# Down-projection weights of a two-layer decoder trunk: their two halves built by GpSimd-issued DMAs instead of by a load and VectorE

## The chip, the cores and the metric

The kernel runs on one core of a Trainium2 chip. TensorE (PE in the profile, with PEld for its weight loads), VectorE (DVE), ScalarE (ACT), GpSimd (POOL) and SyncE (SP, which here only issues DMAs) run side by side, each through its own instruction queue in order, and wait for each other by semaphores. The metric is the device time of one execution in microseconds, lower is better; the time before is the median of three runs.

## What is computed

Two layers over 512 tokens of width 1024, all in float32. Each layer is: half-step SwiGLU FFN, a mixer (layer 0 a Conformer convolution, layer 1 sparse attention), a second half-step SwiGLU FFN, and a gated per-layer embedding; at the end one RMSNorm. Cut to what matters here:

```
def swiglu(x, wg, wu, wd):                 # wg, wu: 1024 x 2816, wd: 2816 x 1024
    return (silu(x @ wg) * (x @ wu)) @ wd

for i in range(2):
    x = x + 0.5 * swiglu(rms_norm(x, ffn1_norm[i]), ffn1_w_gate[i], ffn1_w_up[i], ffn1_w_down[i])
    x = x + (conformer_conv if i == 0 else nsa_mixer)(rms_norm(x, mix_norm[i]), ...)
    x = x + 0.5 * swiglu(rms_norm(x, ffn2_norm[i]), ffn2_w_gate[i], ffn2_w_up[i], ffn2_w_down[i])
    x = x + sigmoid(rms_norm(x, ple_norm[i]) @ ple_w_gate[i]) * (p[i] @ ple_w_in[i])
return rms_norm(x, final_norm)
```

The four FFNs (two a layer) hold four down matrices `w_down`; they are what the change is about.

## The kernel before

**Products.** The matmuls take fp32r, a rounded form of float32. To keep the precision, every operand is split into a high part h (the value rounded to fp32r) and a low part l (the value minus h, rounded), and each product is three matmuls: h·h, h·l and l·h, in this order, in `mm3` (lines 349, 350, 351). The weight block of 128 x 128 is the stationary operand, so lines 349 and 350 load `wh` and line 351 loads `wl`.

**Weights.** The host packs all 128 x 128 weight blocks in the order of use into units of eight (128 x 1024 float32, 512 KB); `plan` lists the units and gives each a kind. Kind "s" is the plain one: `_load` fetches the unit with a DMA from SP's queue into one of two `raw` buffers (line 243), and `_split` lets ScalarE copy it rounded into `wh` (line 291) and VectorE, or GpSimd for some names, subtract `wh` from `raw` into `wl` (line 292). Kinds "a" and "b" are pairs of units of the gate and up matrices; these products go by a seven-product scheme (`pairs`), for which `first_sums` and `combine` form sums of blocks and split them (lines 305 to 324). Kind "r" is loaded raw.

**Buffers and order.** There are five `wh` and five `wl` buffers (HLB = 5), used in rotation by the splits. `block` is asked for each weight block; it calls `ahead`, which writes down the splits up to five entries beyond the one in use (fewer while `held` blocks are still needed) and, through `loads`, the loads of the units that come next. A split can run when the unit that had its buffers five splits earlier is used up. The instructions are written down in this order; when the program is built, a planner with a model of the chip's timing arranges each engine's queue by when it thinks that things are ready, the earlier written first.

**An FFN.** The 22 blocks f of the inner width are cut into parts of 8, 8 and 6. In each part the gate and up products of all its f are computed (in pairs f, f+1, with ScalarE copying sums out of PSUM at line 496 and VectorE adding at line 495 between the products), SiLU and the product with up give `hid` (its split is at lines 551 to 554), and then the down products: for each m of the eight output blocks, sum over the part's f of `w_down[f, m]` times `hid[f]`, 128 x 512 outputs (24 matmuls for a unit of eight blocks). The first two m are interleaved: all but the last two f of m = 0, the same of m = 1, then the last two f of both. VectorE adds each finished m to the residual (lines 605, 606). A part's down blocks are 8 units (6 in the third part), so an FFN has 22 down units and the kernel 88, in twelve parts.

Beside this, GpSimd issues few DMAs of its own (line 1289: eight stores of 256 KB from SBUF to DRAM; some small loads), and it computes the low parts for `ple_w_gate`, `conv_w_pw2` and the attention weights, the reciprocal roots of the norms, and parts of the convolution and the attention.

Of the kernel before, what the change touches and what calls it, by code (L numbers as in the profile page):

```python
# [11 lines left out]
F32 = mybir.dt.float32  # L12
F32R = mybir.dt.float32r
I32 = mybir.dt.int32
AF = mybir.ActivationFunctionType
OP = mybir.AluOpType
# [40 lines left out]
def plan():  # L57
    units, kinds = [[]], ["s"]
    place = {}

    def put(key, rows, cols, kind="s"):
        w = sum(b - a for a, b in cols)
        used = sum(x[2] for x in units[-1])
        if used + w > HU or kinds[-1] != kind:
            units.append([])
            kinds.append(kind)
            used = 0
        place[key] = (len(units) - 1, used, w)
        units[-1].append((key, used, w, rows, cols))

    def ffn(n, i):
        for fs in PARTS:
            order = [(nm, f) for f in fs if f < PLAIN for nm in ("gate", "up")]
            for f in fs:
                if f >= PLAIN and f % 2 == 0:
                    order += [("gate", f), ("gate", f + 1), ("up", f), ("up", f + 1)]
            for nm, f in order:
                for k in range(KD):
                    put((f"ffn{n}_w_{nm}", i, k, f), k, ((f * 128, f * 128 + 128),), "ab"[f % 2] if f >= PLAIN else "s")
            for m in range(KD):  # L80
                for f in fs:
                    put((f"ffn{n}_w_down", i, f, m), f, ((m * 128, m * 128 + 128),))

    def full(name, i, kk, ms):
        for m in ms:
            for k in range(kk):
                put((name, i, k, m), k, ((m * 128, m * 128 + 128),))

    def conv(i):
        for c in range(KD):  # L90
            for o in (c, c + KD):
                for k in range(KD):
                    put(("conv_w_pw1", i, k, o), k, ((o * 128, o * 128 + 128),))
        for z in range(L):
            full("ple_w_in", z, PLE // 128, range(KD))
        for ms in (range(0, 4), range(4, 8)):
            for k in range(KD):
                for m in ms:
                    put(("conv_w_pw2", i, k, m), k, ((m * 128, m * 128 + 128),))

    def nsa():
        def proj(tag, *cols):
            for k in range(KD):
                put(("nsa_w_in", 0, k, tag), k, cols)

        kv = lambda j, g: (QD + j * KV + g * HD, QD + j * KV + g * HD + HD)
        for j in (0, 1):
            for gp in (0, 1):
                proj(("c", j, gp), (QD + j * KV + gp * 128, QD + j * KV + gp * 128 + 128))
            if j == 0:  # L110
                proj("gates", *[(QD + 6 * KV, QD + 6 * KV + 48)] * 2)

        def group(g):
            if g == 0:
                proj(("k", g), kv(2, g), kv(4, g))
            for pr in range(2):
                o = (g * 2 + pr) * 128
                proj(("q", g, pr), (o, o + 128))
            if g > 0:
                proj(("k", g), kv(2, g), kv(4, g))  # L120
            proj(("v", g), kv(3, g), kv(5, g))

        group(0)
        for c in ("k", "v"):
            for kk in range(16):
                for mh in range(2):
                    put((f"nsa_cmp_w{c}1", 0, kk, mh), kk, ((mh * 128, mh * 128 + 128),), "r")
            for mh in range(2):
                put((f"nsa_cmp_w{c}2", 0, mh), mh, ((0, 64), (0, 64)), "r")
        for g in range(1, G):  # L130
            group(g)
        full("nsa_w_out", 0, 4, range(KD))
        for ms in (range(0, 4), range(4, 8)):
            for k, m in [(k, m) for k in range(4, 8) for m in ms] if ms[0] == 0 else [(k, m) for m in ms for k in range(4, 8)]:
                put(("nsa_w_out", 0, k, m), k, ((m * 128, m * 128 + 128),))

    for i in range(L):
        ffn(1, i)
        if i == 0:
            conv(0)  # L140
        else:
            nsa()
        ffn(2, i)
        full("ple_w_gate", i, KD, range(KD))
    return units, kinds, place


UNITS, KINDS, PLACE = plan()
# [41 lines left out]
def drain(gen):  # L190
    for _ in gen:
        pass


class Kern:
# [35 lines left out]
        return (slice(0, w // 2), slice(w // 2, w)) if j == 0 else (slice(0, w),)  # L231

    def _load(self, j):
        if KINDS[j] == "r":
            return
        if KINDS[j] == "b":
            t = self.ptile("rawx", 2, HU)
        else:
            t = self.wpool.tile([128, HU], F32, name=f"raw{j}", tag="raw", bufs=2)
        w = sum(x[2] for x in UNITS[j])  # L240
        self.raw[j] = t
        for c in self.pieces(j, w):
            self.lastload = self.nc.sync.dma_start(t[:, c], self.a["w"][j, :, c]).ins
            yield

    def loads(self):

        while self.next_raw < len(UNITS):
            j = self.next_raw
            if KINDS[j] == "r":  # L250
                if ENTRY[j] > self.next_split:
                    return
            elif BEFORE[j] is not None and LAST[BEFORE[j]] >= self.next_split or KINDS[j] == "b" and not self.here(j):
                return
            drain(self._load(j))
            self.next_raw += 1
# [11 lines left out]
    def _split(self, what, j):  # L268
        nc = self.nc
        w = sum(x[2] for x in UNITS[j])  # L270
        if what == "r":
            t = self.wpool.tile([128, HU], F32, name=f"wr{j}", tag="wh", bufs=self.HLB)
            nc.sync.dma_start(t[:, :w], self.a["w"][j, :, :w])
            self.hl[j] = (t, t)
            return
        if what in "cd":
            self.combine(what, j)
            return
        pair = KINDS[j] == "a"
        t = self.raw[j]  # L280
        if KINDS[j] == "s":
            del self.raw[j]
        h, l = self.halves()
        name = UNITS[j][0][0][0]
        nsa, calm = name.startswith("nsa"), name.startswith(CALM)
        eng = nc.gpsimd if calm or nsa and j % 4 in L_POOL else nc.vector
        for c in self.pieces(j, w):
            if nsa and j % 4 in H_POOL:
                nc.gpsimd.tensor_copy(h[:, c], t[:, c])
            else:  # L290
                nc.scalar.activation(h[:, c], t[:, c], AF.Copy)  # L291
            eng.tensor_tensor(l[:, c], t[:, c], h[:, c].bitcast(F32), op=OP.subtract)  # L292
        self.hl[("s", j) if pair else j] = (h, l)
        if pair:
            self.first_sums(j)
# [1210 lines left out]
```

## Time and profile before

| | |
|---|---|
| median of 3 runs | 2041.17 us (2040.91 to 2041.41) |
| the profiled execution, its own time | 2038.98 us |
| its span, first to last instruction | 2037.2 us |
| mean granted TensorE clock | 0.992 |
| weight units loaded into `raw`, `rawx`, `wr` | 257, 80, 9 |

The page lists per engine the busy time and its share of the span, then groups of instructions by source line: `out<-in`, shapes, count, busy time, mean duration of one in ns, and the idle time of the engine just before them with what ended it. A timeline row gives start (us from the span's start), duration, engine, line, operation and, in brackets, the idle time before and what ended it. In a tile view, three durations are minimum, median and maximum.

### The profile page before, as it was taken

The page shows a single profiled execution, that of the slowest core. Times are in us where ns is not written, and L with a number is a line of the kernel's source. Part 1 is how long each engine was busy: PE and PEld are TensorE (multiplying, and loading weights), DVE is VectorE, ACT ScalarE, POOL GpSimd, SP SyncE. Part 2 cuts the span into 40 slices and gives each one's busy share as a digit, 9 for nine tenths or more (in the row PEclk, how much of TensorE's full clock was granted, in tenths as well). Part 3 has the DMA queues.
Part 4 walks back from the last instruction along what each step waited for, and adds up shares of the span by engine and source line. Part 5 has one row for each costly group of instructions (what it writes and reads, how often), then busy time and mean ns, then how long its engine had stood idle before and what let it go on. Part 6 is the DMA issues. An engine that isn't in the chain of part 4 may idle for free.

```text
span 2037.2 us, 32829 instructions
## 1 busy us (share of the span) xinstructions
PE 1998.5 (98%) x12534; PEld 1794.0 (88%) x12534; DVE 1564.8 (77%) x2767; ACT 1102.2 (54%) x1972; POOL 329.9 (16%) x365
## 2 busy tenths in 40 slices
PE   8999999999999999999999999999999989999998
PEld 6989999888789898988899989888888779898987
DVE  8869777795687796877977868647989797786875
ACT  6636445663565363545644535437888665363543
POOL 0000000352200000021000000557666200000022
PEclk9999999999999999999999999999999999999999
DMA  4323323466325243243232322463332023232241
GB/s 168 104 93 103 125 75 103 180 213 204 125 98 172 92 143 118 96 144 104 83 114 94 114 91 89 159 189 108 90 93 100 27 98 114 94 115 93 88 142 61
DMA packets 79484, 235.16 MB, mean 115 GB/s; under 512 B 8848, under 2 KB 16160, under 8 KB 79328
## 3 DMA queue, kind: packets, MB, share of 16 engines
q1 hardware_dynamic: 78368, 230.69, 34.2%
q8 instruction: 98, 1.61, 0.3%
q0 software_dynamic: 816, 2.33, 0.3%
q14 instruction: 58, 0.48, 0.1%
q10 hardware_dynamic: 144, 0.07, 0.0%
HBM read 214.66 MB, written 16.29 MB: 113 GB/s over the span
## 4 chain that ended last, share of the span: by engine, by line
PE 83%; DVE 9%; ACT 3%; issue 2%; DMA 2%; SPq 0%; POOL 0%; DVEq 0%; ACTq 0%; POOLq 0%
PE b L349 26%; PE b L350 26%; PE b L351 26%; PE b L797 2%; DMA raw<-in_w 1%; DVE t L1221 1%; DVE wl L292 1%; PE b L1156 1%; PE b L1095 1%; DVE t L475 1%; DVE s L408 1%; DVE wl L310 1%; PE b L1218 1%; DVE e L1174 1%; ACT e L1176 0%
## 5 line engine op out<-in xcount | busy, mean ns | idle before, releaser
L349 PE MATMUL b<-s,wh 128*128 128x256 f32 (+1 forms) x1408 | 451.3, 322 | 8.3 <-ACT t L577 6.9
L350 PE MATMUL b<-s,wh 128*128 128x256 f32 (+1 forms) x1408 | 449.8, 320 | 1.3 <-DVE s L408 0.9
L351 PE MATMUL b<-s,wl 128*128 128x256 f32 (+1 forms) x1408 | 449.0, 320 | 0.1
L291 ACT ACTIVATE wh<-raw 128x1024 fp32r<-128x1024 f32 (+1 forms) x251 | 263.9, 1054 | 259.1 <-PE b L350 170.0
L349 PE MATMUL b<-px,wh 128*128 128x256 f32 (+1 forms) x1112 | 321.1, 290 | 6.0 <-ACT px L483 6.0
L350 PE MATMUL b<-px,wh 128*128 128x256 f32 (+1 forms) x1112 | 321.9, 290 | 2.3 <-DVE px L475 2.3
L351 PE MATMUL b<-px,wl 128*128 128x256 f32 (+1 forms) x1112 | 321.6, 290 | 0.0
L292 DVE TENSOR_TENSOR wl<-raw,wh 128x1024 fp32r<-128x1024 f32 (+1 forms) x205 | 251.4, 1228 | 74.9 <-ACT wh L291 74.2
L349 PEld LDWEIGHTS b<-s,wh 128*128 128x128 f32 x1408 | 270.1, 192 | 28.4 <-ACT t L577 7.8
L350 PEld LDWEIGHTS b<-s,wh 128*128 128x128 f32 x1408 | 270.3, 192 | 19.9 <-DVE s L408 2.2
L351 PEld LDWEIGHTS b<-s,wl 128*128 128x128 f32 x1408 | 270.0, 192 | 17.7 <-DVE wl L292 0.5
L351 PE MATMUL b<-hid,wl 128*128 128x512 f32 x704 | 275.3, 393 | 0.0
L350 PE MATMUL b<-hid,wh 128*128 128x512 f32 x704 | 275.1, 392 | 0.0
L349 PE MATMUL b<-hid,wh 128*128 128x512 f32 x704 | 270.4, 390 | 0.0
L292 POOL TENSOR_TENSOR wl<-raw,wh 128x1024 fp32r<-128x1024 f32 (+1 forms) x53 | 128.4, 2427 | 717.2 <-ACT wh L291 717.1
L349 PEld LDWEIGHTS b<-px,wh 128*128 128x128 f32 x1112 | 209.5, 189 | 10.9 <-ACT px L483 6.4
L350 PEld LDWEIGHTS b<-px,wh 128*128 128x128 f32 x1112 | 209.8, 189 | 7.5 <-DVE px L475 2.7
L351 PEld LDWEIGHTS b<-px,wl 128*128 128x128 f32 x1112 | 209.5, 189 | 3.8
L496 ACT ACTIVATE G<-b 128x256 f32<-128x256 f32 x400 | 145.0, 376 | 124.2 <-PE b L351 102.6
L605 DVE SCALAR_TENSOR_TENSOR b<-b,R 128x512 f32<-128x512 f32 x96 | 66.4, 694 | 120.3 <-PE b L351 120.3
L350 PEld LDWEIGHTS b<-hid,wh 128*128 128x128 f32 x704 | 132.3, 188 | 28.8
L349 PEld LDWEIGHTS b<-hid,wh 128*128 128x128 f32 x704 | 132.3, 188 | 28.6
(246 smaller groups left out, 3716.2 us busy)
## 6 DMA issues: line engine op xcount, KB each, us to landing
raw<-in_w SPq DMA_DIRECT2D x255, 512.0 KB, 3.3
rawx<-in_w SPq DMA_DIRECT2D x80, 512.0 KB, 3.2
tw<-in_tw SPq DMA_DIRECT2D x20, 576.0 KB, 6.7
skew<-table SPq DMA_DIRECT2D x16, 320.0 KB, 5.6
z<-t SPq DMA_DIRECT2D x16, 256.0 KB, 2.2
hid<-z SPq DMA_DIRECT2D x16, 256.0 KB, 4.1
tt<-skew SPq DMA_DIRECT2D x16, 256.0 KB, 3.0
wr<-in_w SPq DMA_DIRECT2D x8, 512.0 KB, 4.0
```

The lines of the kernel that those rows point to most:

```text
L291: nc.scalar.activation(h[:, c], t[:, c], AF.Copy)
L292: eng.tensor_tensor(l[:, c], t[:, c], h[:, c].bitcast(F32), op=OP.subtract)
L310: nc.vector.tensor_tensor(l, src, h.bitcast(F32), op=OP.subtract)
L349: mm(out, sh, mh, start=start, stop=False, **how)
L350: mm(out, sh, ml, start=False, stop=False, **how)
L351: mm(out, sl, mh, start=False, stop=stop, **how)
L408: b = nc.vector.scalar_tensor_tensor(view(l), x, g, view(h.bitcast(F32)), op0=OP.mult, op1=OP.subtract)
L475: sub = lambda o, x, y: nc.vector.tensor_tensor(o, x, y, op=OP.subtract)
L496: copy = lambda o, x: nc.scalar.activation(o, x, AF.Copy)
L605: nc.vector.scalar_tensor_tensor(p[m], p[m], 0.5, R, op0=OP.mult, op1=OP.mult)
L797: nc.tensor.matmul(p[:, q * SP:q * SP + SP], T[q][:, d * 128:d * 128 + 128], u[:, q, o:o + SP], start=d == 0, stop=d == LAGS - 1)
L1095: nc.tensor.matmul(P[mh][:, :124], w, B[kk // 4][:, kk % 4, :], start=kk == 0, stop=kk == 15)
```

## The change

The down blocks get a kind of their own, "x". `_load` and `loads` skip such units like those of kind "r", so they have no `raw` buffer. `_split` builds both halves in place: a DMA from GpSimd's queue loads the unit into `wh`, converting to fp32r on the way; ScalarE writes `-wh` into `wl`; a second DMA from GpSimd's queue loads the same unit again and adds it to `wl`.

```diff
-                    put((f"ffn{n}_w_down", i, f, m), f, ((m * 128, m * 128 + 128),))
+                    put((f"ffn{n}_w_down", i, f, m), f, ((m * 128, m * 128 + 128),), "x")
...
-        if KINDS[j] == "r":
+        if KINDS[j] in "rx":
             return
...
-            if KINDS[j] == "r":
+            if KINDS[j] in "rx":
                 if ENTRY[j] > self.next_split:
                     return
...
+            return
+        if what == "x":
+            h, l = self.halves()
+            nc.gpsimd.dma_start(h[:, :w], self.a["w"][j, :, :w])
+            nc.scalar.activation(l[:, :w], h[:, :w].bitcast(F32), AF.Copy, scale=-1.0)
+            nc.gpsimd.dma_start(l[:, :w], self.a["w"][j, :, :w], accum_op=OP.add)
+            self.hl[j] = (h, l)
             return
```

The packing of the units, their number and all matmuls stay the same.

## The prediction

> **What bounds the kernel now.** I read the page's busy shares first, then the groups of the down products, then who PE waited for.
>
> ```profile
> span 2037.2 us, 32829 instructions
> PE 1998.5 (98%) x12534; PEld 1794.0 (88%) x12534; DVE 1564.8 (77%) x2767; ACT 1102.2 (54%) x1972; POOL 329.9 (16%) x365
> PE 83%; DVE 9%; ACT 3%; issue 2%; DMA 2%; SPq 0%; POOL 0%; DVEq 0%; ACTq 0%; POOLq 0%
> L351 PE MATMUL b<-hid,wl 128*128 128x512 f32 x704 | 275.3, 393 | 0.0
> L350 PE MATMUL b<-hid,wh 128*128 128x512 f32 x704 | 275.1, 392 | 0.0
> L349 PE MATMUL b<-hid,wh 128*128 128x512 f32 x704 | 270.4, 390 | 0.0
> ```
>
> PE is busy for 1998.5 of 2037.2 us. The three groups of the down products have no idle time before them at all: not once did PE stand still for a down weight. The chain of waits gives DVE 9%, but that only says which event came last; it is no time that PE lost.
>
> ```profile
> PE b L349 <- ACT t L577: 6.9, 4, 3.9
> PE b L349 <- ACT px L483: 6.0, 2, 3.4
> PE b L350 <- DVE px L475: 2.3, 2, 1.3
> PE b L349 <- ACT wh L291: 0.2, 1, 0.2
> ```
>
> PE's waits (total, times, longest) are at the starts of FFNs (L475, L483, L577: 15.2 us together); a weight split cost it 0.2 us in all. So taking work off VectorE at the down weights has next to nothing to win, and all depends on whether the new way of making the halves is still in time. For that I looked at the second part of the first FFN: the ACT timeline, where a split starts when its buffers come free, and PE's, where the down products start.
>
> ```profile
> 212.57 1.06 ACT L291 ACTIVATE wh<-raw 128x1024 fp32r<-128x1024 f32 x1 [0.43 <-PE b L350]
> 219.58 1.06 ACT L291 ACTIVATE wh<-raw 128x1024 fp32r<-128x1024 f32 x1 [0.40 <-PE b L350]
> 220.94 1.06 ACT L291 ACTIVATE wh<-raw 128x1024 fp32r<-128x1024 f32 x1
> ...
> 259.50 1.06 ACT L309 ACTIVATE wh<-sq 128x1024 fp32r<-128x1024 f32 x1 [4.49 <-PE b L350]
> 264.99 1.06 ACT L309 ACTIVATE wh<-sq 128x1024 fp32r<-128x1024 f32 x1 [4.42 <-PE b L350]
> ```
> ```profile
> 226.51 0.39 PE L349 MATMUL b<-hid,wh 128*128 128x512 f32 x1
> 226.74 0.39 PE L350 MATMUL b<-hid,wh 128*128 128x512 f32 x1
> ...
> 230.63 0.39 PE L349 MATMUL b<-hid,wh 128*128 128x512 f32 x1
> ```
> ```profile
> L351 PEld LDWEIGHTS b<-hid,wl 128*128 128x128 f32 x704 | 132.5, 188 | 27.3
> ```
>
> The splits of the first three down units start at 212.57, 219.58 and 220.94, the first two as soon as PE lets go of the buffers. PE starts a down matmul every 0.23 us, so a unit's 24 take 5.5 us, as the 5.49 us between the splits at 259.50 and 264.99 confirm. The first unit is used from 226.51, the second after 18 matmuls, from 230.63; its low half two matmuls later, and a weight load earlier (188 ns): 230.9. The allowances, from buffers free to low half needed, are therefore 226.5 + 0.3 - 212.6 = 14.2 us for the first unit and **11.3 us for the second**; for the third 226.5 + 11.0 - 220.9 = 16.6 us, since it is used after the two units before it, and more for the later ones. The second unit is the tight one, once in each of the twelve parts.
>
> **The change part by part.** Removed for each of the 88 units: a load on SP's queue, and a subtraction on VectorE.
>
> ```profile
> L291 ACT ACTIVATE wh<-raw 128x1024 fp32r<-128x1024 f32 (+1 forms) x251 | 263.9, 1054 | 259.1 <-PE b L350 170.0
> L292 DVE TENSOR_TENSOR wl<-raw,wh 128x1024 fp32r<-128x1024 f32 (+1 forms) x205 | 251.4, 1228 | 74.9 <-ACT wh L291 74.2
> 160.00:212.00 52.00, 52.00 (x442) 52.00 (x441) 48.43 (x71) 32.97 (x56) 0.00 (x0) 1.00 0.32 108
> 227.00:270.00 43.00, 43.00 (x189) 35.31 (x188) 28.51 (x37) 12.23 (x14) 0.00 (x0) 1.00 0.26 86
> ```
>
> VectorE loses 88 x 1.228 = 108 us. In the two stretches (length, then busy PE, PEld, DVE, ACT, POOL, clock, DMA share, GB/s: a pair phase and a down phase) VectorE works 48.4 of 52 us and 28.5 of 43, but PE works all of both, so the 108 us hide behind PE and I count nothing for them. ScalarE's rounding copy becomes a negation of the same shape: 1.06 us for 1.06 us. Freed `raw` buffers let the next part's loads go earlier; those splits do not hold PE now, so that is nothing either.
>
> Added: 176 DMAs on GpSimd's queue. GpSimd is idle in both stretches (0.00), so the issues are hidden as work; what counts is their latency.
>
> ```profile
> q1 hardware_dynamic: 78368, 230.69, 34.2%
> raw<-in_w SPq DMA_DIRECT2D x255, 512.0 KB, 3.3
> z<-t SPq DMA_DIRECT2D x16, 256.0 KB, 2.2
> xd<-s POOLq DMA_DIRECT2D x8, 256.0 KB, 2.9
> L1289 POOL DMA_DIRECT2D xd<-s x8: 539/557/610, 1286.7 to 1314.7; - x8
> 1278.00:1306.00 28.00, 28.00 (x124) 23.01 (x123) 22.33 (x26) 10.24 (x15) 11.64 (x9) 1.00 0.42 135
> ```
>
> - The loading DMA. A plain 512 KB load from SP lands 3.3 us after its issue. The 256 KB stores take 2.9 us from GpSimd against 2.2 from SP, so I add 0.7: **4.0 us**. No row shows a converting DMA. Below, it is as fast as SP's (3.3); above, it takes 6.7, as if its data had to go through twice at full latency. I stay at 4.0, as the bytes moved are those of the 3.3 us row.
> - The negation: **1.06 us**, plus 0.1 for the hops between queues.
> - The accumulating DMA. It reads the unit and the destination. SP's queue moved 230.69 MB in 34.2% of 16 engines' span, 697 us, so 512 KB (0.524 MB) keep 16 engines busy for 1.6 us. A second stream is 1.6 us more, and its descriptors, if as many again, another 0.5 us of issue (557 ns for 128 rows): 4.0 + 1.6 + 0.5 = **6.1 us**. Again no row shows it: below 4.0 (the second stream is free), above 8.0 (two whole transfers in a row). I take the sum of the terms, which is also the middle.
> - Company on the DMA engines: the third unit's load is issued 1.4 us behind the second's, the fourth's and fifth's beside the second's accumulation, 1.6 us of engine time each. I count half of one, **0.8 us**.
>
> Sum for the second unit: 4.0 + 1.06 + 0.1 + 6.1 + 0.8 = 12.1 us against 11.3: late by 0.8 us, and PE stands still for that, in each of twelve parts: **9.6 us**. The first unit (12.1 of 14.2) and those from the third on (16.6 and more) are in time. With both DMAs at their lower ends (3.3 + 4.0) the sum is 9.3 and nothing is late; with both at the upper (6.7 + 8.0) it is 16.7: the second unit is 5.4 us late, the first 2.5 us, which delays the second's need as well, so 5.4 us a part and 65 us in all.
>
> The Trainium skill speaks of the second stream: "Collectives: The Full Stack", section "The bandwidth ceiling: the fold count and why AG ≠ RS ≠ AR", has a reduction by DMA at 32.35 GB/s where a copy has 62.28, because it reads two sources. By it the term of 1.6 us would be an estimated 1.5 us and the whole 8 us. No run here shows it yet.
>
> Two queues get a wait. ScalarE's negation waits for the loading DMA, with the PSUM copies of L496 and the splits of the pairs behind it; PE needs such a copy two products of 12 matmuls later:
>
> ```profile
> 218.81 0.28 PE L349 MATMUL b<-px,wh 128*128 128x256 f32 x1
> ...
> 219.61 0.28 PE L350 MATMUL b<-px,wh 128*128 128x256 f32 x1
> ```
> ```profile
> L496 ACT ACTIVATE G<-b 128x256 f32<-128x256 f32 x400 | 145.0, 376 | 124.2 <-PE b L351 102.6
> ```
>
> Seven steps of PE between the two rows make 0.114 us each, so 24 make 2.7 us, less 0.4 us for the copy itself: 2.3 us of patience. GpSimd's accumulating issue waits for ScalarE, with the next unit's load behind it. Whether that load must wait depends on the planned order. I take it that the planner lets it go first when its buffers are free first, since VectorE's queue shows it doing so:
>
> ```profile
> 245.67 0.69 DVE L320 TENSOR_TENSOR sq<-raw,rawx 128x512 f32<-128x512 f32 x1
> ...
> 247.12 0.69 DVE L305 TENSOR_TENSOR sq<-rawx,raw 128x512 f32<-128x512 f32 x1
> ...
> 250.50 1.22 DVE L292 TENSOR_TENSOR wl<-raw,wh 128x1024 fp32r<-128x1024 f32 x1
> ```
>
> L305 of the later `combine`, and L320, ran before the L292 that is written ahead of them. If instead load and accumulation alternated strictly, a unit would take 4.0 + 1.06 + 0.56 = 5.6 us of GpSimd's queue against PE's 5.5, just even.
>
> **Rivals.**
> - *Hidden anyway* (chance 0.36). The accumulating DMA lands within 5.3 us, or has no company; the chain ends inside 11.3 us. For it: the lower bounds give 9.3. Time 2041, no change.
> - *ScalarE blocked* (0.06). The plan puts the negation where a faster DMA would have landed; the copies of L496 stand behind it beyond the 2.3 us that PE tolerates. At 1 us for each of the first three units of twelve parts: 36 us, 2077. Against it: ScalarE now waits up to 6.7 us for a raw load and PE never noticed.
>
> ```profile
> ACT wh L291 <- DMA raw<-in_w: 71.9, 33, 6.7
> ```
>
> - *VectorE blocks the issue* (0.04). Each of the two issues sits behind one 1.22 us VectorE instruction: 2.4 us more on the chain, 12 x (0.8 + 2.4) = 38 us, 2079. Against it: the eight issues of L1289 took 539 to 610 ns while VectorE was busy for 22.3 of 28 us. The Trainium skill has the rule ("SBUF — State Buffer", section "SBUF: two separate sides"): GpSimd cannot write DMA descriptors while VectorE holds their shared port in a two-port mode; the rows just named do not show it.
> - *Slow arithmetic in the DMA* (0.12). If adding costs twice what I take, 12.2 us, the chain is 18.2 us, 6.9 us late, 83 us, 2124. From a unit's 5.5 us of engine time on (3.2 by my terms plus 1.6 for the load), every unit would be late and the time open upward.
> - *The other side: faster* (0.08). VectorE's freed 108 us let the plan put the work at the FFN starts earlier, and half of the 15.2 us of waits there goes: 2033. It decides if the splits of L475 and L483 are late because of VectorE's backlog; against it, no down unit is near those places.
> - *It does not round.* If the converting DMA left the value whole, the low half would be zero; the matmuls take the same time, so this has no price and no chance of its own.
>
> **How the numbers follow.** The forecast, a late second unit, has 0.34: 2038.98 + 9.6 = 2048.6 by the profiled execution; that stands 2.2 us under the median of 2041.17, so the median should become 2050.8, rounded to **2050**. A measurement of this kernel can tell about 0.2%, 4 us, from no change. Faster 0.08, same 0.36, slower 0.34 + 0.06 + 0.04 + 0.12 = 0.56. The range goes from 2036 to 2122: it holds the forecast, the hidden case, both blocked cases and the upper ends of the unknown costs (2041 + 65 = 2106), and leaves out most of the fast and the slow rival. The forecast's own range is 2045 to 2065.
>
> **What would show it.** After: L292 on DVE 88 fewer, DVE near 1457 us; 88 more ScalarE activations on `wl`; two groups of 88 GpSimd DMAs, whose landing times (4.0 and 6.1 here) settle the main term; idle time before L351 with `hid,wl`, about 10 us in twelve waits, released by a DMA on `wl`. Zero there means the hidden case; idle before the pair products released by ACT L496, the blocked case; idle in the later units of a part, the slow one. I am wrong at the root if PE waits anywhere else for more than a few us.

## The result, and the profile after

| | before | after |
|---|---|---|
| median of the runs | 2041.04 us (4 runs) | 2061.13 us (2053.49, 2060.57, 2061.69, 2063.59) |
| ratio after to before | | 1.0092, 95% interval 1.008 to 1.0105 |
| the same kernel once more | 2041.16 us (21 runs) | 2061.38 us (4 runs); ratio 1.0101, interval 1.0087 to 1.0115 |
| profiled run, and its span | 2038.98, 2037.2 us | 2053.49, 2051.7 us |

The change makes the kernel about 20 us slower, 1%. The forecast was slower by 9.6 us. The first profiled run after the change was the shortest of its eight by 7 us, so it shows only part of the loss; the trace of the second run of the same kernel (span 2059.3 us) shows the rest.

The page of the kernel after: busy shares and DMA queues (packets, MB, share of 16 engines), the groups of the changed lines, and the landing times.

```profile
PE 2003.2 (98%) x12534; PEld 1794.3 (87%) x12534; DVE 1466.3 (71%) x2679; ACT 1095.9 (53%) x1972; POOL 456.6 (22%) x541
q1 hardware_dynamic: 65696, 184.55, 27.1%
q0 software_dynamic: 26160, 94.61, 20.0%
L358 PE MATMUL b<-hid,wl 128*128 128x512 f32 x704 | 272.0, 392 | 9.1 <-DMA wl<-in_w 9.1
L279 ACT ACTIVATE wl<-wh 128x1024 fp32r<-128x1024 f32 x88 | 93.3, 1060 | 270.2 <-DMA wh<-in_w 269.9
L299 DVE TENSOR_TENSOR wl<-raw,wh 128x1024 fp32r<-128x1024 f32 (+1 forms) x117 | 143.7, 1230 | 82.8 <-ACT wh L298 82.5
wh<-in_w POOLq DMA_DIRECT2D x88, 512.0 KB, 6.1
wl<-in_w POOLq DMA_DIRECT2D x88, 512.0 KB, 5.5
```

L358 is the low-part matmul that was L351. It had no idle time before; now it has 9.1 us, all released by a DMA on `wl`. VectorE's subtractions are 88 fewer (205 to 117, 107.7 us less), and nothing was won with them. The rounding DMA lands after 6.1 us in the median where I had put 4.0, the accumulating one after 5.5 where I had put 6.1. Next, PE's longest waits (total, times, longest) and one of ScalarE's.

```profile
PE b L358 <- DMA wl<-in_w: 9.1, 7, 2.3
PE b L356 <- ACT t L584: 7.1, 4, 4.2
PE b L356 <- ACT px L490: 4.6, 2, 2.5
...
PE b L356 <- ACT s L414: 1.2, 1, 1.2
...
ACT wl L279 <- DMA wh<-in_w: 269.9, 70, 9.7
```

The waits at the FFN starts (L584, L490) are the old ones; the first row is new. L414, at the start of the attention, has grown: before, the same wait (L407) was 0.5 us. To see how the 9.1 us arise, here is the chain of waits in the seventh part, from the release of the second unit's buffer on (start, length, what).

```profile
1043.30 0.49 POOL wl L280
1043.79 5.85 DMA wh<-in_w
...
1051.08 7.21 DMA wl<-in_w
1058.29 0.04 issue
1058.34 0.50 PE b L358
```
```profile
1043.80:1058.30 14.50, 12.21 (x81) 10.86 (x79) 7.63 (x13) 6.70 (x10) 4.87 (x8) 1.00 0.91 203
```

Between the landing of `wh` (1049.64) and the issue at 1051.08 lie ScalarE's negation of 1.06 us and some 0.3 us until GpSimd issues. The whole chain takes 14.5 us, and PE stood still for the last 2.3. The second fence is the view by windows for that stretch: the second number from the right is the time of the DMA packets begun in the stretch, as a share of 16 engines, 0.91. (In the stretches of before in the prediction it was 0.26 to 0.42. Packets that end after the stretch count whole, so it can pass 1.) L280's 0.49 us ahead of the chain is the first unit's accumulating DMA, issued just before on the same queue.

PE's own order has changed as well. Here is its timeline ahead of that wait, from the second unit's first matmul on.

```profile
1054.47 0.39 PE L356 MATMUL b<-hid,wh 128*128 128x512 f32 x1
1054.70 0.39 PE L357 MATMUL b<-hid,wh 128*128 128x512 f32 x1
1054.93 0.39 PE L356 MATMUL b<-hid,wh 128*128 128x512 f32 x1
1055.16 0.39 PE L357 MATMUL b<-hid,wh 128*128 128x512 f32 x1
1055.39 0.40 PE L356 MATMUL b<-hid,wh 128*128 128x512 f32 x1
1055.62 0.39 PE L357 MATMUL b<-hid,wh 128*128 128x512 f32 x1
1058.34 0.50 PE L358 MATMUL b<-hid,wl 128*128 128x512 f32 x1 [2.33 <-DMA wl<-in_w]
```

Three blocks' matmuls on the high half run before the first on the low half. In before that one was always the 21st of a part's down products. The planner has moved it to the 25th place, in the parts of six f to the 29th; only the fourth part keeps the 21st. So PE needs the low half 12.0 to 12.5 us after the rounding DMA's issue, 13.2 to 13.4 in the parts of six f, and not after 11.3.

Where the loss lies along the kernel is seen by comparing the start of the same matmul, by its number in PE's order, in two traces. The table gives how much PE's delay against the first trace of before grows, in us: over the twelve parts' down products (from 144 matmuls ahead of a part's first, where both kernels have the same order, to its last), over the attention (from the ninth part's end to before's 1622 us), and in all, for the two traces of the kernel after and for the runs of the next section.

```
kernel                   each of the 12 parts                               parts  attention  all
after                    2.0 1.5 1.1 -.2  .4  .1 2.5 2.3  .1  .9 1.1  .1    12.0      3.6    14.5
after, once more         1.7 1.9  .9 -.1  .2  .1 5.7 3.8  .1  .8 1.3  .1    16.5      3.7    22.0
second unit old          -.1  .1  .1 1.7  .1  .1 -.1  .1  .1  .6  .1  .1     3.1      4.8     9.6
second unit alone         .0  .1  .1  .0  .1  .1  .0  .1  .1  .0  .1  .1     0.6      6.4    10.5
no accumulation          -.1  .1  .1  .3  .1  .1 -.1  .1  .2  .1  .1  .1     1.2      0.9     3.6
accumulation alone       1.2  .0  .0  .7  .0  .0  .0  .0  .0  .1  .0  .0     2.0      0.4     2.7
first unit old            .8  .9  .1  .0 1.5  .2  .1 1.9  .1  .0 1.2  .4     7.0     10.5    19.9
swapped                  1.0 3.0 2.0  .3 1.2 1.6 1.2 1.7 1.7 1.7 2.3 1.8    19.5      0.1    20.9
last part old too        -.1  .1  .1 -.1  .1  .1 -.1  .1  .0  .0  .1  .1     0.6      1.1     1.7
h one unit ahead          .0  .7  .1 1.3  .1  .1  .2 1.3  .2 1.8  .1  .1     5.8     10.5    16.7
before, sixth buffer     -.2  .0  .0 -.2  .0  .0 -.2  .0  .0  .0  .0  .0    -0.5     10.4    11.2
```

In the two traces of the changed kernel 83% and 75% of the loss lie in the down products, and most of the rest in the attention, where no down weight is made.

### The profile page after: what moved, and what is told of

It reads as the page before. It is cut to its first block, busy times and chain, and to the rows that moved or that the text cites. A ratio compares the mean times of both kernels' runs of the same rounds, so it can differ in the third digit from the quotient of the medians.

```text
span 2051.7 us, 32921 instructions
## 1 busy us (share of the span) xinstructions
PE 2003.2 (98%) x12534; PEld 1794.3 (87%) x12534; DVE 1466.3 (71%) x2679; ACT 1095.9 (53%) x1972; POOL 456.6 (22%) x541
## 4 chain that ended last, share of the span: by engine, by line
PE 78%; DVE 9%; DMA 5%; issue 5%; ACT 3%; POOL 0%; SPq 0%; DVEq 0%; POOLq 0%; ACTq 0%
PE b L358 24%; PE b L356 24%; PE b L357 24%; DMA wl<-in_w 2%; PE b L804 2%; DMA wh<-in_w 2%; DVE t L1228 1%; PE b L1163 1%; PE b L1102 1%; PE b L1225 1%; DVE s L415 1%; DVE wl L299 1%; DVE e L1181 1%; DMA raw<-in_w 0%; DVE acc L432 0%
## 5 line engine op out<-in xcount | busy, mean ns | idle before, releaser
L358 PE MATMUL b<-s,wl 128*128 128x256 f32 (+1 forms) x1408 | 448.0, 319 | 0.1
L358 PE MATMUL b<-px,wl 128*128 128x256 f32 (+1 forms) x1112 | 319.6, 289 | 0.0
L358 PEld LDWEIGHTS b<-s,wl 128*128 128x128 f32 x1408 | 269.1, 191 | 17.9 <-DVE wl L299 0.5
L358 PE MATMUL b<-hid,wl 128*128 128x512 f32 x704 | 272.0, 392 | 9.1 <-DMA wl<-in_w 9.1
L278 POOL DMA_DIRECT2D wh<-in_w x88 | 58.8, 680 | 849.3 <-PE b L358 405.1
L279 ACT ACTIVATE wl<-wh 128x1024 fp32r<-128x1024 f32 x88 | 93.3, 1060 | 270.2 <-DMA wh<-in_w 269.9
L298 ACT ACTIVATE wh<-raw 128x1024 fp32r<-128x1024 f32 (+1 forms) x163 | 169.5, 1048 | 100.0 <-PE b L357 55.5
L358 PEld LDWEIGHTS b<-px,wl 128*128 128x128 f32 x1112 | 208.7, 188 | 4.3
L299 DVE TENSOR_TENSOR wl<-raw,wh 128x1024 fp32r<-128x1024 f32 (+1 forms) x117 | 143.7, 1230 | 82.8 <-ACT wh L298 82.5
L358 PEld LDWEIGHTS b<-hid,wl 128*128 128x128 f32 x704 | 132.2, 188 | 40.6 <-DMA wl<-in_w 12.5
```

The source lines that it names most:

```text
L278: nc.gpsimd.dma_start(h[:, :w], self.a["w"][j, :, :w])
L279: nc.scalar.activation(l[:, :w], h[:, :w].bitcast(F32), AF.Copy, scale=-1.0)
L358: mm(out, sl, mh, start=False, stop=stop, **how)
```

## The experiments

The theory, T1: the loss is the second unit of each part, whose chain of two DMAs, one behind the other, does not fit into its allowance of some 11.4 us (in before's order of PE). The rivals: a loss with every DMA on GpSimd's queue, or by the planner's new order of work (T2); the third unit late as soon as the second is not (T3). In the diffs, `_p` is a unit's place in its part and `_q` the part's number, both from 0.

**The second unit the old way.**

```diff
...
+        if _p == 1:
+            KINDS[_j] = "s"
```

> The second down unit of each of the twelve parts is made the old way (load on SP's queue, ScalarE's rounding copy, VectorE's subtraction); the other 76 stay with the two GpSimd DMAs. Theory T1 (the whole loss is the second unit's low half landing after PE needs it): the idle time before the down matmul on the low half (9.1 us after the change) falls to under 2 us, PE's stalls from 63.9 to about 51 us, and the median to 2041 to 2046 us. Rival T2 (the loss comes with every DMA on GpSimd's queue, or from the planner's new order of work): 76 of the 88 units stay, so at least 76/88 of the 20 us stay, 2058 us or more. Rival T3 (the third unit is late as soon as the second no longer is): the idle time moves to the third unit and the median stays above 2050.

Measured: 2047.55 us (ratio 1.0031, interval 1.0019 to 1.0042). Twelve units of 88 give back two thirds of the loss, as T1 has it and T2 has not; T3 falls, as the idle time before the low half is down to 1.0 us. But the median is 1.5 us above T1's band, and the table shows where: the parts' 12.0 to 16.5 us went down to 3.1, while the attention's share stayed, 4.8. Something is lost there that no second unit makes.

**The second unit alone.**

```diff
...
+        if _p != 1:
+            KINDS[_j] = "s"
```

> Only the second down unit of each part is made by the two GpSimd DMAs, the other 76 the old way. T1 with company as its cause (the second unit's rounding DMA lands in 6.1 us instead of 3.4 because it is issued right behind the first unit's accumulating DMA): without that company the landing falls to about 3.4 to 4.0 us, the chain to some 10.5 us, and the median to 2041 to 2046. T1 without company (the two DMAs are that slow by themselves): the landings stay at 6 and 5.5 us and most of the 20 us stays, 2053 to 2061. T2 (loss per DMA): 12/88 of it, 2044.

Measured: 2044.71 us (1.0022, 1.0012 to 1.0032). The page's landing times:

```profile
wh<-in_w POOLq DMA_DIRECT2D x12, 512.0 KB, 3.6
wl<-in_w POOLq DMA_DIRECT2D x12, 512.0 KB, 6.7
```

Without its neighbours' GpSimd DMAs the rounding DMA lands after 3.6 us, and no wait of PE on `wl` is left. The accumulating one, with plain loads of the next units beside it, takes 6.7. The chain of both has 11.8 us in the mean, 1.2 less than after the change, but over 11.4 in eight parts: it is in time there because the planner has moved the first matmul on this low half to the 30th or 35th place in ten parts, which leaves 13.1 to 14.2 us. So fewer neighbours and a later need both have a share in it. What this trace loses (it is the longest of nine runs) lies in the attention, 6.4 us, and 0.6 us in the parts, so T2's 2044 fits the median but not the place. T2's turn to be tried comes with the next run.

**No accumulating DMA.**

```diff
-            nc.gpsimd.dma_start(l[:, :w], self.a["w"][j, :, :w], accum_op=OP.add)
```

> The accumulating DMA is left out, so the low halves are minus the high halves and the output is not the reference's; the rounding DMA, ScalarE's negation and everything else stay. T1: the second unit is ready some 6 us earlier, nothing is late at the down products, median 2041 to 2044; if the accumulating DMA is the company that stretches the rounding DMA, its landing falls from 6.1 to 4 us or less; if not, it stays near 6. T2 (planner's order, GpSimd's queue): half of the DMAs are left, so some 10 us of the 20 stay, 2051.

Measured: 2042.29 us (1.0005, 0.9996 to 1.0014), no difference that can be told, and 9 us under what T2 gives.

```profile
wh<-in_w POOLq DMA_DIRECT2D x88, 512.0 KB, 3.6
q0 software_dynamic: 13488, 48.47, 7.7%
```

The low halves are then minus the high halves, so the output is not the reference's. All 88 rounding DMAs are there, on the same queue, and land after 3.6 us in the median. It is the accumulating DMAs that stretch them to 6.1. PE has before's order here (21st place in every part), so this run also measures the prediction's allowance: in eleven parts of twelve the second unit's low half was ready 4.5 to 5.5 us after its buffers came free, and 5.8 to 6.9 us before PE needed it, 11.2 to 11.4 us in all (13.0 in the fourth part).

**The accumulating DMA alone.** The high half is loaded and rounded the old way.

```diff
...
+            t = self.raw.pop(j)
...
-            nc.gpsimd.dma_start(h[:, :w], self.a["w"][j, :, :w])
+            nc.scalar.activation(h[:, :w], t[:, :w], AF.Copy)
```

> The high half is made the old way (load on SP's queue into the raw buffers, ScalarE's rounding copy); ScalarE then negates it into the low buffer, and the raw weights are added there by the accumulating DMA as after the change. VectorE stays free of the 88 subtractions. T1 (two landings in a row are what does not fit): the chain is 1.06 + 1.06 + 0.3 + 5.5 to 7.5 = 8 to 10 us of the 11.4 allowed, nothing is late at the down products, median 2042 to 2047 (the attention's start may still lose up to 5). Rival (the accumulating DMAs are what hurts, by whatever they share): 2055 or more.

Measured: 2043.12 us (1.0012, 1.0003 to 1.0021).

```profile
wl<-in_w POOLq DMA_DIRECT2D x88, 512.0 KB, 8.1
q0 software_dynamic: 13488, 48.47, 12.7%
```

Here the accumulating DMA takes even longer, 8.1 us, beside the plain loads that run ahead, and still nearly nothing is late (2.0 us in the parts): a chain with one landing in it has room. So it is the two landings in a row, each stretched by the neighbours, that do not fit. VectorE is as free in this kernel as after the change (1461.4 us busy), and it is no faster than before.

The two q0 rows give the price of each DMA in time of the 16 engines. In before GpSimd's queue took 0.3% of the span, 6 us. The 88 rounding DMAs alone: 7.7% of 2040.9 us, less 6, by 88 = 1.7 us each. The 88 accumulating ones: 12.7% of 2039.9 us, less 6, by 88 = 2.9 us each. A plain load took 1.6 us by the prediction's row. The two prices add up: 88 times 4.6, and 6, is 411 us, and the kernel after has 20.0% of 2051.7 us, 410.

**What the company is: the first unit the old way, and the order swapped.** These two ask whether the second unit's rounding DMA is held up by the first unit's accumulating DMA just ahead of it.

```diff
...
+        if _p == 0:
+            KINDS[_j] = "s"
```

> The first down unit of each part is made the old way; the second and all later ones keep the two GpSimd DMAs. T1 with company as its cause: with no accumulating DMA of a first unit just ahead of it, the second unit's rounding DMA lands in 3.6 to 4 us instead of 5.8, its chain falls from 13.0 to 11 to 11.5 us against 11.4 allowed, and the median to 2044 to 2050. Rival T6 (what stretches it is the GpSimd DMAs as a whole, or the accumulating DMA is too slow in any company): 76 units remain as they were, the second unit stays late by 1.5 us, median 2057 or more.

```diff
-            nc.gpsimd.dma_start(h[:, :w], self.a["w"][j, :, :w])
+            first = nc.gpsimd.dma_start(h[:, :w], self.a["w"][j, :, :w]).ins
+            if self.late:
+                with self.tc.issue_after(first):
+                    self.add(*self.late.pop())
...
-            nc.gpsimd.dma_start(l[:, :w], self.a["w"][j, :, :w], accum_op=OP.add)
+            if KINDS[j - 1] != "x":
+                self.late.append((l, j, w))
+            else:
+                self.add(l, j, w)
...
```

> All 88 units as after the change; only the order on GpSimd's queue differs: the second unit's rounding DMA is issued ahead of the first unit's accumulating DMA. If a DMA is held up by what was issued ahead of it on that queue (T1 with a queue as the mechanism), the second unit's rounding DMA lands in 3.6 to 4.2 us and its chain fits, 11.0 to 11.5; the first unit's low half lands 1 to 2 us later, within its spare 0.1 to 4 us in nine or ten parts of twelve; median 2045 to 2053. If the two share the DMA engines whichever goes first (T1 with bandwidth as the mechanism), the rounding DMA still takes 5 us or more, and the median stays at 2056 to 2063.

Measured: 2058.04 us (1.0077, 1.0064 to 1.0089) with the first unit old, 2061.36 us (1.0095, 1.0079 to 1.011) swapped. Both times missed what the first guess of each gave and lie where the second had put them (2057 or more; 2056 to 2063), though the landing that I had named went where the first had it. With the first unit old, more than half of the loss is in the attention (10.5 us); the parts went from 12.0 down to 7.0. The second unit's chain, means over the twelve parts, in us from issue to landing (the chain has 1.4 us more, for ScalarE and the hops):

```
kernel               rounding DMA   accumulating DMA   chain
after                    5.80             5.80          13.0
first unit old           4.05             6.84          12.4
swapped                  4.19             7.77          13.4
second unit alone        3.77             6.65          11.8
```

What is issued ahead on GpSimd's queue does hold up what comes behind it: with the first unit's accumulation gone or behind, the rounding DMA lands 1.6 to 1.75 us earlier. But the next DMA then takes 1.0 to 2.0 us longer. In the swapped kernel the first unit's accumulating DMA, which used to land after 5.2 to 6.2 us, mostly takes about 8, and now the first units are late as well:

```profile
PE b L367 <- DMA wl<-in_w: 13.9, 13, 1.6
```

L367 is that kernel's low-part matmul: thirteen waits instead of seven, 19.5 us in the parts. As far as these runs show, the queue's order only decides which DMA pays, and the sum is set by the DMA engines, 91% in use in the window shown above, all of it by GpSimd's queue:

```profile
q0 software_dynamic: 797, 2.94, 91.2%
```

91.2% of 14.5 us is 13.2 us of engine time inside one second unit's chain; its own two DMAs are 1.7 + 2.9 = 4.6 of it, the neighbours' 8.6.

**The rounding DMA one unit ahead.** A sixth buffer for the high halves, and the rounding DMA of a unit issued with the unit before it.

```diff
+        if e < len(SPLITS) and self.next_split == e and SPLITS[e][0] == "x" and SPLITS[e][1] not in self.first:
+            self.first[SPLITS[e][1]] = self.begin(SPLITS[e][1])
...
-            h, l = self.halves()
-            nc.gpsimd.dma_start(h[:, :w], self.a["w"][j, :, :w])
+            h = self.first.pop(j, None) or self.begin(j)
+            l = self.wpool.tile([128, HU], F32R, name=f"wl{self.uid}", tag="wl", bufs=self.HLB)
+            self.uid += 1
...
```

> The high halves get a sixth buffer, and the rounding DMA of a down unit is issued one unit ahead of its negation and accumulation, so that it no longer stands in the second unit's chain: from the release of the low buffer that chain is negation 1.06 and accumulating DMA some 5.5 to 7 us, 8 of the 11.3 us allowed. T1: nothing is late, median 2041 to 2045. If the accumulating DMAs, now with more rounding DMAs beside them, stretch beyond 10 us, some of the loss stays, 2046 to 2055. T2 (loss per DMA, or by the planner's order): 2058 or more, as after the change.

Measured: 2056.48 us (1.0079, 1.0065 to 1.0093), far above what T1 gives and just under T2's. The second unit is in time in every part, by 0.6 to 4.0 us, and no wait on `wl` is left. Still the kernel is only 5 us faster than the one after the change. In its place PE waits for ScalarE's copies out of PSUM (L516, the old L496), which now stand behind negations that wait 3.3 to 3.9 us for their rounding DMA:

```profile
PE b L369 <- ACT G L516: 3.5, 4, 1.1
```

That is the prediction's rival of a blocked ScalarE, in another kernel; it accounts for part of the 5.8 us in the parts. The larger loss, 10.5 us, lies in the attention. Its control is before with the sixth buffer and nothing else:

```diff
-        h = self.wpool.tile([128, HU], F32R, name=f"wh{self.uid}", tag="wh", bufs=self.HLB)
+        h = self.wpool.tile([128, HU], F32R, name=f"wh{self.uid}", tag="wh", bufs=self.HLB + 1)
...
```

> The kernel before, with a sixth buffer for the high halves and nothing else. A control for the run that issued the rounding DMA one unit ahead: there no down unit was late, and yet it lost 15.6 us, of which 10.7 between 1269 and 1565 us, in the attention, where no down weight is made. If the sixth buffer (by the order that the planner then makes) is the cause, this kernel loses 8 to 12 us there as well, 2049 to 2053; if the DMAs are the cause, it stays at 2041.

Measured: 2050.94 us (1.0045, 1.0031 to 1.0059), 10.4 us of it in the attention. So those 10.5 us come with the buffer and not with any DMA; that they come by the order of work that the planner makes with it is a reading, not shown. Up to half of them is TensorE's clock: in the control's trace it stood at 0.50 three times in the attention, for 3.4 us each, from 1315.3, 1397.2 and 1544.0 us (worth up to 5.1 us), and here twice, from 1399.6 and 1549.8. Between these two kernels the DMAs cost 5.5 us.

**The last part before the attention the old way too.** Now for the attention's 3.6 to 6.4 us in the other runs. The timeline shows GpSimd's last store ahead of it, of before and of after (start, length):

```profile
1314.68 0.56 POOL L1289 DMA_DIRECT2D xd<-s  x1
```
```profile
1302.43 0.91 POOL L280 DMA_DIRECT2D wl<-in_w  x1 [3.92 <-ACT wl L279]
...
1325.37 0.56 POOL L1296 DMA_DIRECT2D xd<-s  x1
```

It comes 10.7 us later than before, where PE had lost 7.9 us when the ninth part ended. GpSimd's queue holds the stores and low halves of the attention's start, behind the last part's DMAs.

The edit is shown against the run with the second units old.

```diff
...
-        if _p == 1:
+        if _p == 1 or _q == 8:
             KINDS[_j] = "s"
```

> The second unit of every part and all six units of the last part before the attention are made the old way; 66 units keep the two GpSimd DMAs. Kept with only the second units old, PE lost 5 us between 1269 and 1416 us, where GpSimd's queue holds the low halves and stores of the attention's start behind the last part's DMAs. Theory T4 (that loss comes from this one part): it goes, median 2042 to 2044.5. Rival T2' (the rest of the loss comes a little from every unit): 66 of 76 units remain, 2046 to 2047.5.

Measured: 2044.22 us (1.0014, 1.0005 to 1.0023), 3.3 us less than with the second units alone the old way, from one part of twelve. The attention's loss in the trace fell from 4.8 to 1.1 us. (Up to 1.7 of the 4.8 is the clock, at 0.50 for 3.4 us from 1317.7, behind a wait of 1.45 us.) Not 66 units, as expected above, but 71 still take the new way, and they lose 0.6 us in the parts together. Why the run with the first unit old loses 10.5 us there, and the swapped one 0.1, I did not follow up. The trace of the former has two waits of 1.96 us for ScalarE at the attention's start, at 1321 and 1325 us, and the clock at 0.50 for 6.8 us from 1323.7; the planner's order differs in each.

**The kernel after once more.** The runs of the changed kernel lie up to 10 us apart, those of before 5 (2038.75 to 2043.56 over all sets).

> The kernel after the change, unaltered, for a second trace: its first profiled run (2053.5 us) was the shortest of four, the others took 2060.6 to 2063.6. T1: a longer run is longer by later second units, so the idle time before the down matmul on the low half grows with the run's time: about 9 us at 2053, 15 to 17 at 2061, because the rounding DMA of the second unit lands later still (6 to 7 us in the mean instead of 5.8). Rival T5: the extra time of the longer runs lies outside the down products, and that idle time stays near 9 us whatever the run takes.

Measured: 2061.38 us; this time the profiled run was a typical one, 2061.03 us.

```profile
PE b L358 <- DMA wl<-in_w: 9.2, 7, 2.7
```

The idle time is the same as in the short run, 9.2 us, and so are the chains (12.9 us in the mean): T1's guess on the spread is wrong, and the rival T5 is half right: the idle time stays, but 4.5 us of the 7.5 between the two traces do lie in the down products, behind the waits. The table has 3.2 us more in the seventh part and 1.5 in the eighth. PE's timeline and the windows of the seventh part, first of this trace:

```profile
1060.77 0.80 PE L358 MATMUL b<-hid,wl 128*128 128x512 f32 x1 [2.72 <-DMA wl<-in_w]
...
1061.79 0.63 PE L357 MATMUL b<-hid,wh 128*128 128x512 f32 x1
1062.21 0.63 PE L358 MATMUL b<-hid,wl 128*128 128x512 f32 x1
```
```profile
1061.00:1062.00 1.00, 1.00 (x3) 0.81 (x4) 0.00 (x0) 0.00 (x0) 0.00 (x0) 0.50 1.03 283
1062.00:1064.00 2.00, 2.00 (x6) 1.54 (x6) 0.00 (x0) 0.00 (x0) 0.00 (x0) 0.50 1.01 246
1064.00:1066.00 2.00, 2.00 (x6) 1.59 (x5) 0.00 (x0) 0.86 (x1) 0.00 (x0) 0.50 0.88 182
1066.00:1068.00 2.00, 2.00 (x8) 1.61 (x7) 0.00 (x0) 0.19 (x1) 0.86 (x1) 0.79 0.19 39
```

Then of the short run:

```profile
1058.34 0.50 PE L358 MATMUL b<-hid,wl 128*128 128x512 f32 x1 [2.33 <-DMA wl<-in_w]
1058.67 0.39 PE L356 MATMUL b<-hid,wh 128*128 128x512 f32 x1
1058.90 0.40 PE L357 MATMUL b<-hid,wh 128*128 128x512 f32 x1
```
```profile
1059.00:1061.00 2.00, 2.00 (x11) 1.62 (x10) 0.00 (x0) 0.00 (x0) 0.00 (x0) 1.00 1.08 272
```

After a wait of 2.72 us TensorE's granted clock (third number from the right) was 0.50 for some 6 us, and the matmuls started every 0.42 us instead of 0.23. After a wait of 2.33 us at the same place it stayed at 1.00. Half the clock for some 6 us costs 3 us, more than the wait itself. The eighth part has the other 1.5 us: behind a wait of 1.77 us the clock was 0.50 for 3.4 us, and in the short run, behind a longer wait of 1.92 us at the same place, it was not. The windows just behind these waits, of this trace and of the short run:

```profile
1190.00:1195.00 5.00, 5.00 (x17) 3.98 (x16) 0.00 (x0) 1.06 (x1) 0.15 (x1) 0.69 1.04 232
```
```profile
1185.00:1190.00 5.00, 5.00 (x23) 4.12 (x22) 0.69 (x1) 1.06 (x1) 0.52 (x1) 1.00 1.00 234
```

So the length of the wait alone does not decide it. The Trainium skill speaks of such a gate ("TensorE: Matmul & The Clock Gate", section "Part 1: The HAM clock gate"): an idle window of about 3.4 us halves the clock, and the window runs free of the program. That the clock falls to half, and in one run and not in another, agrees; that waits of 2.72 and 1.77 us were enough is less than a whole window.

## Why the prediction was half right

- **VectorE's 108 us are worth nothing**: right. 107.7 us went, PE's work stayed, and with the accumulation alone, where VectorE is as free, the kernel is not faster.
- **The second unit is the tight one; allowance 11.3 us**: right. Measured 11.2 to 11.4 us in eleven parts, but in before's order of PE's matmuls. The prediction took that order as fixed; in the changed kernel the allowance was 12.0 to 13.4 us. The units from the third on were in time, the first one too by 0.0 to 4.1 us.
- **Landing times of 4.0 and 6.1 us**: both too long for a DMA by itself. The rounding one takes 3.6 us without accumulating DMAs beside it, the accumulating one 5.1 to 5.4 at its best. The engine time behind them was about right: 1.7 and 2.9 us measured, 1.6 and 3.2 put. The hops, put at 0.1 us, took 0.3.
- **Company, 0.8 us: the mis-sized term of the chain.** I counted half a load of 1.6 us. The undisturbed chain is 3.6 + 1.4 + 5.2 = 10.2 us (10.3 measured in the fourth part), and it would have fitted; the measured mean is 13.0, so the company costs 2.8. As the DMAs by themselves were put too long, the whole chain came out only 0.9 us longer than the 12.1 of the sum. I had left out the first unit's accumulating DMA, issued 0.8 us ahead of the second's rounding DMA and worth 2.9 us of the engines, and had counted the rounding DMAs of the third to fifth units as if they found the engines free. In the window shown they were 91% in use.
- **Late by 0.8 us in twelve parts, 9.6 us**: PE waited 9.1 and 9.2 us for the DMA in the two traces, in seven parts. That this meets the 9.6 is luck: a chain 0.9 us longer than put stood against an allowance 0.7 to 2.1 us longer.
- **PE stands still for the lateness, and for nothing else: the step that failed.** The prediction put the price of a wait at its length and all other losses at nothing; this is what takes 9.6 us to 20. Each wait with the clock at 1.00 behind it delayed PE by some 0.28 us more than it lasted (2.61 for the 2.33 of the seventh part, by the starts of the same matmuls), 2 us in all, as matmuls of 0.39 us that start every 0.23 lose their overlap; with small shifts of the order the parts lost 12.0 us. In a typical run the clock was halved behind two of the waits, which makes the 12.0 us 16.5.
- **Nothing late elsewhere**: the other half of that step, wrong by 3.6 us, at the attention's start, where GpSimd's queue has other work. The prediction saw that queue idle in two stretches, and read the stores between 1278 and 1306 us only for the time of their issue.
- **The profiled run stands 2.2 us under the median**: this held for before; after the change it was 7.6, mostly for the clock's reason: of the 7.5 us between its two traces 4.5 lie in the parts, behind those two waits.
- **The rivals**: none was seen in the changed kernel. PE waited there for no copy out of PSUM (ScalarE blocked); the accumulating DMA at its best is a sixth faster than I had put it (slow arithmetic). The waits at the FFN starts, 15.2 us before, are 13.7 and 14.4 in the two traces, so half of them did not go (the faster side). As to VectorE blocking the issue, here is the group of the rounding DMA's issues (busy time, mean ns of one, idle time before): 0.68 us in the mean, against 0.53 without accumulating DMAs, and none is longer by a VectorE instruction of 1.22 us.

```profile
L278 POOL DMA_DIRECT2D wh<-in_w x88 | 58.8, 680 | 849.3 <-PE b L358 405.1
```

The Trainium skill's price of the second stream ("Collectives: The Full Stack", section "The bandwidth ceiling: the fold count and why AG ≠ RS ≠ AR") was 62.28 to 32.35, a ratio of 1.9, an estimated 1.5 us. The engine times measured here are 2.9 and 1.7 us: a ratio of 1.7, and 1.2 us for the second stream.

None of the kernels tried beats the one before.

## What to carry to other kernels

Before chaining two DMAs inside the time that a buffer is free, add up the engine time of all DMAs that run in that time, the neighbours' and the one issued just ahead among them, and not only the latency of one's own: here 4.6 us of own work stood beside 8.6 us of others' in 14.5. Moving work off an engine that isn't the bound was worth nothing here, and its price was the chain that it made longer. A wait of TensorE of 2 to 3 us can cost twice its length, by the clock behind it, in one run and not in the next. And an allowance read off a trace holds only as long as the planner keeps the order that it was read from.

## What the runs showed of the hardware

- An accumulating DMA of 512 KB keeps the 16 engines busy for 2.9 us and a rounding one for 1.7 (a plain load 1.6); at their best they land after 5.1 to 5.4 and 3.4 to 3.6 us. After the change single ones took up to 10.4 and 9.6.
- On GpSimd's queue a DMA is held up by the one issued ahead of it: with the order swapped, the rounding DMA went from 5.8 to 4.2 us, the accumulating one behind it from about 5.4 to 8.
- The granted clock fell to 0.50 for some 6 us after a wait of 2.72 us, and did not after one of 2.33 us at the same matmul in another run; at another matmul it fell for 3.4 us after 1.77 us, and did not after 1.92.
- One more buffer, with no other change, cost the kernel before 9.8 us, nearly all of it in the attention; up to 5.1 us of that by three stretches of the clock at 0.50.
